# Banded attention on column halves, up-projection sums in one PSUM bank, an exchanged copy of a state-space map, reordered stick sums

## The chip, the cores and the metric

The kernel runs on one core of a Trainium2 chip. The metric is the device time of one execution in microseconds (us). The kernel before took 3503.58 us, the median of three runs (3499.01 to 3504.58).

## The reference, cut to what matters

Two transformer blocks, one after the other, on `x` of shape [1, 1024, 1024] in float32. Only the parts that the change touches are shown.

```python
# block 1: x += g_a * concat(mlstm, window_attention) @ w_out;  then a conv-GLU FFN
def window_attention(q, k, v, k_ctx, v_ctx, sink):     # 8 query heads, 2 key/value heads, 64 wide
    s_band = where(|i - j| <= 128, q . k, -inf)         # blocks of 128 queries, 3 blocks of keys
    s_ctx  = q . k_ctx                                  # 256 context keys
    p = softmax(concat([s_band, s_ctx, sink]))
    return p_band @ v + p_ctx @ v_ctx
def conv_glu(h, w_up, conv_w, conv_b, w_down):
    a, val = split(h @ w_up, 2)                         # 1024 -> 2 * 2816
    return (gelu(dwconv(a)) * val) @ w_down
# block 2: pool, dilated attention, stick-breaking attention and s5 branches, gated merge, SwiGLU FFN
def stick_breaking_attention(qkv):                      # 4 heads of 128
    log_not = where(mask, log_sigmoid(-z), 0)
    excl = reversed_cumsum(log_not) - log_not
    w = where(mask, exp(log_sigmoid(z) + excl), 0);  return w @ v
def s5_mixer(u, ...):                                   # 32 groups of 16 channels, 64 complex states
    h_t = lam_bar * h_(t-1) + b_bar @ u_t;  y = Re(c @ h) + d * u
h = silu(gu[:, :2816]) * gu[:, 2816:];  x = x + h @ w_down
```

## The kernel before

Activations lie transposed in SBUF: the 1024 features as eight tiles of 128 partitions, with the 1024 tokens along the free dimension, often cut in a left and a right half of 512. A large product is split by `split` (L378 to L388) into a rounded part `wh`/`bh` and a rest `wl`/`bl` of type fp32r, and `gemm` (L350 to L362) sums three products of these parts (L358, L360, L362). ScalarE makes the rounded part (L382) and VectorE the rest (L383). A product of plain fp32 operands is run by TensorE as two passes, and the trace lists each pass as one matmul record.

PSUM holds two tiles `mm` of two banks (`pmm`) and four tiles `ax` of one bank (`pax`). A scheduler sets the order of each engine's instructions; the code gives it generators which it runs in turns, and the pools' buffer counts decide when a tile can be written again.

**Up-projection** (`factors`, `pair`, `up`). Each 2x2 block product is done by seven half-size products instead of eight (B11, B21, T1, B22, T2, T3, T4). `factors` makes the right-hand factors from the normalised activations and `pair` the left-hand ones from the weights (`combine`, on GpSimd, L892). Every product of a pair is 4 x 3 matmuls of 128x512 and has its own PSUM bank; what is common to several results is added in SBUF: on VectorE (L900) and, for two of the seven sums, on GpSimd. A block has 22 pairs. The first two pairs run in step, since their factors are still being made; from the third on, each pair follows the one before. The norm of the right token half multiplies by the row `r` in SBUF, on VectorE for the first four tiles (L824 in block 1, L822 in block 2), on GpSimd for the last four.

**Banded attention** (`window`). There are 16 units: eight query blocks n, each for two key/value heads v. A unit makes the scores of four query heads (L1191, L1194), the softmax (L1204 to L1216), and then `values`: each block of 128 probabilities is transposed (L1229, fp32), copied to SBUF by VectorE or ScalarE (`pt`, L1232, L1234) and multiplied with 64 columns of `va` (L1236). Unit v writes to partitions 64v to 64v+63 of the bank `pv`, so it uses one half of TensorE's columns. After v = 1, L1247 spreads the reciprocal denominators with 64-column matmuls. The mLSTM runs alongside, with L1412 spreading a row of `Mn` over the partitions.

**State space** (`s5`, the loop around L2132). Per group of channels the map `RT` [128 x 128] is applied to `U` (L2132), and once more with its two column halves exchanged, as two 64-column matmuls (L2133, L2134) into the two halves of `p2`.

**Stick** (L1649 to L1673). Per key block four running sums are added in the bank `zz` before the exponential.

Of the kernel before, what the change touches and what calls it, by code (L numbers as in the profile page):

```python
# [255 lines left out]
class Kern:  # L256
# [183 lines left out]
    def rstd(self, out, acc):  # L440
        nb = out.shape[-1] // P
        y = self.rstd_tokens(acc)
        for b in range(0, nb, 4):
            n = min(4, nb - b)
            self.bcast(out[:, b * P : (b + n) * P], y[:, b : b + n])
        return self.lastr
# [365 lines left out]
    def finish(self, xs, out, gain):  # L812
# [5 lines left out]
        def norm(k, sl, eng):  # L818
            x = xs[k][:, sl]
            g, s = gain(k)  # L820
            if s is None:
                nc.vector.scalar_tensor_tensor(x, x, g, r[:, sl], ALU.mult, ALU.mult)  # L822
            else:
                eng.tensor_tensor(x, x, r[:, sl], ALU.mult)  # L824
                nc.scalar.activation(x, x, AF.Identity, scale=g, bias=s)

        B = {}
        for sl in (L, R):
# [10 lines left out]
            self.rstd(r[:, sl], acc[:, sl])  # L839
        return xd, B, self.factors(xs, B, norm)  # L840


    def factors(self, xs, B, norm):
# [13 lines left out]
        for k, (x, y) in enumerate(pairs):  # L857
            norm(k, R, nc.vector)
# [23 lines left out]
    def pair(self, fp, wa, wv, B, act):  # L882
# [3 lines left out]
        w2 = fp.tile([P, D], F32, tag="w2", name=self.nm("w2"), bufs=2)  # L886
# [3 lines left out]
        def combine(x, y, op):  # L890
            t = fp.tile([P, HT], F32, tag="ws", name=self.nm("ws"), bufs=4)
# [3 lines left out]
        def prod(ps, w, b):  # L895
            hi, lo = self.split_w(w)
            self.gemm(hi, lo, [(ps,) + B[b]])
            return ps

        add = lambda out, x, y, eng=nc.vector: eng.tensor_tensor(out, x, y, ALU.add)  # L900
        copy = lambda x, ps: nc.scalar.activation(x, ps, AF.Copy)
        ps = self.pmm()
        a = fp.tile([P, T], F32, tag="a", name=self.nm("a"), bufs=2)
        v = fp.tile([P, T], F32, tag="v", name=self.nm("v"), bufs=2)
        a0, a1, v0, v1 = a[:, 0:HT], a[:, HT:T], v[:, 0:HT], v[:, HT:T]
# [26 lines left out]
    def up(self, fp, W, B, steps, act):  # L932
        out = []
        run = lambda j: self.pair(fp, W[j], W[NF + j], B, lambda a, v: out.append(self.spill("y", act(j, a, v))))
        g = [run(0), run(1)]
# [6 lines left out]
        next(g[0])  # L942
        cur = g[1]
        for j in range(2, NF):
# [197 lines left out]
    def window(self, ep, qd, kd, kcd, va):  # L1142
# [76 lines left out]
        def values(n, v, ss, rd):  # L1219
            lo_, hi_ = span(n)  # L1220
            nk = 2 + hi_ - lo_
            hp = slice(64 * v, 64 * v + 64)
            if v == 0:
                self.pv = self.pax()
            pv = self.pv
            for k in range(nk):
                pt = self.pax()
                for j in range(4):
                    nc.tensor.transpose(pt[:, j * P : (j + 1) * P], ss[j][:, k * P : (k + 1) * P], ID)  # L1229
                t = self.wp.tile([P, 512], F32, tag="wh", name=self.nm("pt"), bufs=4)  # L1230
                if self.u % 4 == 2 or (self.u % 4 < 2 and k % 2):
                    nc.vector.tensor_copy(t, pt)  # L1232
                else:
                    nc.scalar.activation(t, pt, AF.Copy)  # L1234
                vb = va[k] if k < 2 else va[2 + lo_ + k - 2]
                self.late.append(lambda k=k, vb=vb, t=t: nc.tensor.matmul(pv[hp, :], lhsT=vb[:, hp], rhs=t, start=k == 0, stop=k == nk - 1))  # L1236
                while len(self.late) > 2:
                    self.late.pop(0)()

            while self.late:  # L1240
                self.late.pop(0)()
            if v:

                rb = self.pax()
                for g, r in enumerate((self.r0, rd)):
                    for j in range(4):
                        nc.tensor.matmul(rb[64 * g : 64 * g + 64, j * P : (j + 1) * P], lhsT=r[:, j : j + 1].to_broadcast([P, 64]), rhs=ID, start=True, stop=True)  # L1247
                rs = self.sm.tile([P, 512], F32, tag="junk", name=self.nm("rs"), bufs=1)
                nc.scalar.activation(rs, rb, AF.Copy)
                for j in range(4):  # L1250
                    t = slice(j * P, (j + 1) * P)
                    nc.vector.tensor_tensor(q[j][:, n * P : (n + 1) * P], pv[:, t], rs[:, t], ALU.mult)
            else:
                self.r0 = rd

        self.late = []
        self.qt = queries(*units[0])
        ss = scores(*units[0])
        for i, u in enumerate(units):
            self.u = i  # L1260
            nxt = scores(*units[i + 1]) if i < 15 else None
            values(*u, *ss)
# [11 lines left out]
    def mlstm(self, ep, km, kc, qm, vx, so, G):  # L1274
# [49 lines left out]
        nc.tensor.transpose(q[:, 0:128], Mn, ID)  # L1324
        nc.tensor.matmul(q[:, 128:256], lhsT=m0c.to_broadcast([P, P]), rhs=ID, start=True, stop=True)
# [20 lines left out]
        for h in range(4):  # L1346
# [56 lines left out]
            for half in range(2):  # L1403
# [4 lines left out]
                for d in range(2):  # L1408
                    pd = self.pax()
                    for j in range(4):  # L1410
                        c = col(d, blk(d, half * 4 + j + 2), h)
                        nc.tensor.matmul(  # L1412
                            pd[:, j * P : (j + 1) * P],
                            lhsT=self.c("nident")[:, c : c + 1].to_broadcast([P, P]),
                            rhs=Mn,
                            start=j == 0,
                            stop=False,
                            skip_group_check=True,
                        )
# [66 lines left out]
    def block1_ffn(self, xd, B, steps):  # L1486
        nc, tc, A = self.nc, self.tc, self.A
        with tc.tile_pool(name="f1", bufs=1) as fp:
# [3 lines left out]
            def act(j, a, v):  # L1492
# [6 lines left out]
                nc.vector.tensor_tensor(y[:, 0:HT], y[:, 0:HT], v[:, 0:HT], ALU.mult)  # L1499
                nc.gpsimd.tensor_tensor(y[:, HT:T], y[:, HT:T], v[:, HT:T], ALU.mult)  # L1500
                return y

            yd = self.up(fp, A["w_up"], B, steps, act)
# [88 lines left out]
    def stick(self):  # L1592
# [36 lines left out]
        with tc.tile_pool(name="sb", bufs=1) as fp:  # L1629
# [8 lines left out]
            def chain(h, Q, qh, ql, kh, kl, po, o):  # L1638
# [3 lines left out]
                for kb in range(kb1, -1, -1):  # L1642
# [22 lines left out]
                    if kb < kb1:  # L1665
                        pv()
                    mm(zz, ntril, Lh)
                    mm(zz, ntril, Ll, stop=kb == kb1)
                    if kb < kb1:
                        mm(zz, nones, Sh[:, c0:HT])  # L1670
                        mm(zz, nones, Sl[:, c0:HT], stop=True)
# [234 lines left out]
    def s5(self):  # L1906
# [4 lines left out]
        with tc.tile_pool(name="s5", bufs=1) as fp:  # L1911
# [143 lines left out]
            for q in range(4):  # L2055
# [32 lines left out]
                RT = v8(self.big("RT"))  # L2088
# [287 lines left out]
```

## Time and profile before

| | |
|---|---|
| median of three runs | 3503.58 us |
| the profiled execution, its span | 3506.94 us, 3505.2 us |
| mean granted TensorE clock | 0.988 |
| busy: TensorE, VectorE, ScalarE, GpSimd | 3355.7, 2239.1, 1280.0, 883.7 us |

Stages on the clock of the span, in us: projections 40 to 334, banded attention and mLSTM 334 to 600, up-projection 705 to 1138, stick 1497 to 1690, dilated attention 1763 to 2106, state space 2110 to 2460, second up-projection 2783 to 3215. A matmul record of 128x512 fp32r lasts about 0.39 us, though the next one starts earlier, because matmuls are pipelined; so a cost on TensorE is read from start to start, not from the duration of a record.

### The profile page before, as it was taken

The page shows a single profiled execution, that of the slowest core. Times are in us where ns is not written, and L with a number is a line of the kernel's source. Part 1 is how long each engine was busy: PE and PEld are TensorE (multiplying, and loading weights), DVE is VectorE, ACT ScalarE, POOL GpSimd, SP SyncE. Part 2 cuts the span into 40 slices and gives each one's busy share as a digit, 9 for nine tenths or more (in the row PEclk, how much of TensorE's full clock was granted, in tenths as well). Part 3 has the DMA queues.
Part 4 walks back from the last instruction along what each step waited for, and adds up shares of the span by engine and source line. Part 5 has one row for each costly group of instructions (what it writes and reads, how often), then busy time and mean ns, then how long its engine had stood idle before and what let it go on. Part 6 is the DMA issues. An engine that isn't in the chain of part 4 may idle for free.

```text
span 3505.2 us, 42846 instructions
## 1 busy us (share of the span) xinstructions
PE 3355.7 (96%) x15763; PEld 2644.2 (75%) x15763; DVE 2239.1 (64%) x4041; ACT 1280.0 (37%) x2410; POOL 883.7 (25%) x642
## 2 busy tenths in 40 slices
PE   6999998989999999899999999999999989999998
PEld 4797776768888777677777778777878768888767
DVE  8746776598787797667332227456265685555786
ACT  5224555443333333345232332222222333333332
POOL 3200000056555451200000002221032164544540
PEclk9999999999999999999999999999999999999999
DMA  6545111512222422200121212222464322223222
GB/s 234 193 157 174 37 52 49 174 66 79 88 75 75 165 91 85 102 25 33 54 67 46 68 57 93 70 92 75 152 228 165 126 91 84 79 84 129 94 92 78
DMA packets 139953, 348.61 MB, mean 99 GB/s; under 512 B 16712, under 2 KB 41696, under 8 KB 139744
## 3 DMA queue, kind: packets, MB, share of 16 engines
q1 hardware_dynamic: 139744, 345.88, 29.2%
q8 instruction: 124, 2.03, 0.2%
q14 instruction: 85, 0.70, 0.1%
HBM read 270.67 MB, written 75.16 MB: 99 GB/s over the span
## 4 chain that ended last, share of the span: by engine, by line
PE 80%; DVE 12%; issue 2%; DMA 2%; ACT 2%; POOL 1%; SPq 0%; DVEq 0%; ACTq 0%; POOLq 0%
PE mm L358 15%; PE mm L360 15%; PE mm L362 15%; PE ax L362 6%; PE ax L360 6%; PE ax L358 6%; DVE bl L383 2%; PE ax L1236 2%; PE ax L1649 1%; DVE wl L383 1%; PE ax L1582 1%; PE ax L1584 1%; PE ax L1583 1%; PE mm L1649 1%; PE ax L1229 1%
## 5 line engine op out<-in xcount | busy, mean ns | idle before, releaser
L382 ACT ACTIVATE wh<-w 128x512 fp32r<-128x512 f32 (+1 forms) x508 | 308.3, 610 | 1073.8 <-PE mm L360 693.0
L383 DVE TENSOR_TENSOR wl<-w,wh 128x512 fp32r<-128x512 f32 (+1 forms) x508 | 371.6, 736 | 436.3 <-ACT wh L382 393.7
L362 PE MATMUL ax<-bh,wl 128*128 128x512 f32 x928 | 369.9, 400 | 15.2 <-DVE wl L383 15.1
L360 PE MATMUL ax<-bl,wh 128*128 128x512 f32 x928 | 369.7, 398 | 5.9 <-DVE bl L383 5.7
L358 PE MATMUL ax<-bh,wh 128*128 128x512 f32 x928 | 368.4, 398 | 4.6 <-ACT bh L382 4.6
L358 PE MATMUL mm<-bh,wh 128*128 128x512 f32 x864 | 328.1, 401 | 16.7 <-DVE x L2317 6.5
L362 PE MATMUL mm<-bh,wl 128*128 128x512 f32 x864 | 321.0, 396 | 3.8 <-DVE wl L383 3.6
L360 PE MATMUL mm<-bl,wh 128*128 128x512 f32 x864 | 323.1, 395 | 0.0
L358 PE MATMUL mm<-xh,wh 128*128 128x512 f32 x944 | 311.1, 404 | 2.3 <-DVE sql L386 1.8
L362 PE MATMUL mm<-xh,wl 128*128 128x512 f32 x944 | 312.6, 403 | 0.0
L360 PE MATMUL mm<-xl,wh 128*128 128x512 f32 x944 | 305.0, 401 | 0.0
L383 DVE TENSOR_TENSOR wl<-ws,wh 128x512 fp32r<-128x512 f32 x176 | 215.5, 1234 | 32.3 <-ACT wh L382 31.9
L892 POOL TENSOR_TENSOR ws<-w 128x512 f32<-128x512 f32 x44 | 83.9, 1907 | 579.0 <-DMA w<-in_w_up_dram 508.6
L362 PEld LDWEIGHTS ax<-bh,wl 128*128 128x128 f32 x928 | 176.9, 191 | 59.7 <-DVE wl L383 19.0
L358 PEld LDWEIGHTS mm<-bh,wh 128*128 128x128 f32 x864 | 162.2, 188 | 73.4 <-DVE x L2317 12.1
L360 PEld LDWEIGHTS ax<-bl,wh 128*128 128x128 f32 x928 | 176.2, 190 | 51.8 <-DVE bl L383 11.0
L358 PEld LDWEIGHTS ax<-bh,wh 128*128 128x128 f32 x928 | 176.6, 190 | 46.2 <-ACT bh L382 6.1
L362 PEld LDWEIGHTS mm<-xh,wl 128*128 128x128 f32 x944 | 176.4, 188 | 44.5 <-issue 5.8
L358 PEld LDWEIGHTS mm<-xh,wh 128*128 128x128 f32 x944 | 174.3, 188 | 46.3 <-issue 6.3
L360 PEld LDWEIGHTS mm<-xl,wh 128*128 128x128 f32 x944 | 177.9, 189 | 40.9 <-issue 1.5
L362 PEld LDWEIGHTS mm<-bh,wl 128*128 128x128 f32 x864 | 162.6, 188 | 45.5 <-DVE wl L383 7.0
L360 PEld LDWEIGHTS mm<-bl,wh 128*128 128x128 f32 x864 | 162.9, 189 | 35.0
(636 smaller groups left out, 7101.9 us busy)
## 6 DMA issues: line engine op xcount, KB each, us to landing
w<-in_w_up_dram SPq DMA_DIRECT2D x88, 512.0 KB
wa<-in_w_ada_dram SPq DMA_DIRECT2D x64, 512.0 KB
w<-in_w_out_dram SPq DMA_DIRECT2D x32, 512.0 KB
w<-in_w_gate_dram SPq DMA_DIRECT2D x32, 512.0 KB
gd<-gf SPq DMA_DIRECT2D x32, 512.0 KB
g<-gd SPq DMA_DIRECT2D x32, 512.0 KB
y<-y SPq DMA_DIRECT2D x28, 512.0 KB
w<-in_w_down_dram SPq DMA_DIRECT2D x24, 512.0 KB
```

Source lines behind the costliest of these rows:

```text
L358: nc.tensor.matmul(ps, lhsT=wh, rhs=xh[k], start=s, stop=False, **kw)
L360: nc.tensor.matmul(ps, lhsT=wh, rhs=xl[k], start=False, stop=False, **kw)
L362: nc.tensor.matmul(ps, lhsT=wl, rhs=xh[k], start=False, stop=e, **kw)
L382: first = nc.scalar.activation(hi, src, AF.Copy)
L383: nc.vector.tensor_tensor(lo, src, hi.bitcast(F32), ALU.subtract)
L892: nc.gpsimd.tensor_tensor(t, x, y, op)
L1229: nc.tensor.transpose(pt[:, j * P : (j + 1) * P], ss[j][:, k * P : (k + 1) * P], ID)
L1236: self.late.append(lambda k=k, vb=vb, t=t: nc.tensor.matmul(pv[hp, :], lhsT=vb[:, hp], rhs=t, start=k == 0, stop=k == nk - 1))
L1582: nc.tensor.matmul(ps, lhsT=a, rhs=wh[k], start=k == 0, stop=False)
L1583: nc.tensor.matmul(ps, lhsT=a, rhs=wl[k], start=False, stop=False)
L1584: nc.tensor.matmul(ps, lhsT=b, rhs=wh[k], start=False, stop=k == KC - 1)
L1649: mm = lambda out, lhsT, rhs, **k: nc.tensor.matmul(out, lhsT=lhsT, rhs=rhs, **{"start": False, "stop": False, "skip_group_check": True, **k})
```

## The change

- `window`: the unit v = 0 is only transposed and copied (`turned`); its products wait until v = 1 is turned too, and `product` then issues for each block k the two products, one per column half. The denominators of the two heads alternate as well. The copies of v = 0 go to five buffers of their own.
- `pair`: B11, T2, T3 and T4 are summed in one bank `pa`, T1 and B22 in one bank `pb`. What stands there after B11, T1, T2 and T3 is copied out or added to SBUF before the next product is summed on top; the last sum is read from PSUM by the gate multiplication. Additions on GpSimd fall away, and `up` starts with three pairs in step.
- `factors`: the first four right-half norms read the row from the PSUM tile in which it was made (`rstd` returns it).
- `s5`: `RS`, a copy of `RT` with halves exchanged, is made by 16 more ScalarE copies, and L2133/L2134 become one 128-column matmul.
- The stick's `nones` products precede `pv()`; the mLSTM row becomes two fp32r products of a split `Mn`; a DMA scratch area gets smaller.

```diff
@@ bcast, rstd, factors
+        return ps[:, : nb * P]
-        return self.lastr
+        return row
-                nc.vector.scalar_tensor_tensor(x, x, g, r[:, sl], ALU.mult, ALU.mult)
+                nc.vector.scalar_tensor_tensor(x, x, g, row, ALU.mult, ALU.mult)
-                eng.tensor_tensor(x, x, r[:, sl], ALU.mult)
+                eng.tensor_tensor(x, x, row, ALU.mult)
-            norm(k, R, nc.vector)
+            norm(k, R, nc.vector, row)
@@ pair
+        if first is None:
+            ps = self.pmm()
+            pa, pc = ps[:, 0:HT], ps[:, HT:T]
+        else:
+            pa, pc = first
...
-        copy(a0, prod(ps[:, 0:HT], a11, "B11"))
+        prod(pa, a11, "B11", last=False)
+        copy(a0, pa)
         yield
-        p2 = prod(ps[:, HT:T], a12, "B21")
+        prod(pc, a12, "B21")
+        add(a0, pc, a0)
         yield
-        copy(v1, prod(self.pax(), s1, "T1"))
+        pb = self.pax()
+        prod(pb, s1, "T1", last=False)
+        copy(v1, pb)
+        s4 = combine(a12, s2, ALU.subtract)
         yield
-        s4 = combine(a12, s2, ALU.subtract)
-        add(a1, prod(self.pax(), s4, "B22"), v1)
-        yield
-        add(v0, prod(self.pax(), s2, "T2"), a0)
-        add(a0, p2, a0)
-        add(v1, v1, v0, nc.gpsimd)
-        add(a1, a1, v0, nc.gpsimd)
+        def p3():
+            prod(pb, s4, "B22", first=False)
+        def p6():
+            prod(pa, s2, "T2", first=False, last=False)
+            copy(a1, pa)
...
+        add(a1, pb, a1)
+        y = hidden(a) if first is None else None
         yield
-        s3 = combine(a11, a21, ALU.subtract)
-        p7 = prod(self.pax(), s3, "T3")
-        add(v1, p7, v1)
-        add(v0, p7, v0)
+        prod(pa, s3, "T3", first=False, last=False)
+        add(v1, pa, v1)
         yield
-        add(v0, prod(self.pax(), a22, "T4"), v0)
-        act(a, v)
+        prod(pa, a22, "T4", first=False)
+        out(y or hidden(a), pa, v1)
@@ up
+        def gated(y, v0, v1):
+            nc.vector.tensor_tensor(y[:, 0:HT], y[:, 0:HT], v0, ALU.mult)
+            nc.vector.tensor_tensor(y[:, HT:T], y[:, HT:T], v1, ALU.mult)
+        p, q = self.pmm(), self.pmm()
+        g = [run(0, (p[:, 0:HT], q[:, HT:T])), run(1, (p[:, HT:T], None)), run(2, (q[:, 0:HT], None))]
-        g = [run(0), run(1)]
@@ window
+            def product(k, t1):
+                vb = va[k] if k < 2 else va[2 + lo_ + k - 2]
+                for v, t in enumerate((t0[k], t1)):
+                    hp = slice(64 * v, 64 * v + 64)
+                    nc.tensor.matmul(pv[hp, :], lhsT=vb[:, hp], rhs=t, start=k == 0, stop=k == nk - 1)
...
+            if v == 0:
+                t0, r0 = [turned(n, 0, ss[0], k) for k in range(blocks(n))], ss[1]
+            else:
+                values(n, t0, ss[0], (r0, ss[1]))
@@ s5
-                        R = RT[:, 4 * j + g, :]
-                        nc.tensor.matmul(p1[:, o], lhsT=R, rhs=U[:, 4 * j + g, :], start=True, stop=True)
-                        nc.tensor.matmul(p2[0:64, o], lhsT=R[:, 64:128], rhs=U[:, 4 * j + g, :], start=True, stop=True)
-                        nc.tensor.matmul(p2[64:128, o], lhsT=R[:, 0:64], rhs=U[:, 4 * j + g, :], start=True, stop=True)
+                        for p, R in ((p1, RT), (p2, RS)):
+                            nc.tensor.matmul(p[:, o], lhsT=R[:, 4 * j + g, :], rhs=U[:, 4 * j + g, :], start=True, stop=True)
```

The first place is TensorE's order in the banded attention, at the end of unit n = 2. In the kernel before, `pt` are the turned probabilities of head v = 1, L1229 the transposes, L1247 the denominators:

```order
L1236 MATMUL ax_3505<-pt_3661,va_1271 64x512
L1229 MATMUL ax_3679<-const,ws_3463 128x128
L1229 MATMUL ax_3679<-const,ws_3472 128x128
L1229 MATMUL ax_3679<-const,ws_3481 128x128
L1229 MATMUL ax_3679<-const,ws_3490 128x128
L1236 MATMUL ax_3505<-pt_3668,va_1331 64x512
L1247 MATMUL ax_3689<-const,rden_3316 64x128 x4
L1236 MATMUL ax_3505<-pt_3676,va_1361 64x512
L1236 MATMUL ax_3505<-pt_3684,va_1391 64x512
L1247 MATMUL ax_3689<-const,rden_3503 64x128 x4
```

In the changed kernel L1259 are the transposes and L1282 the products; of the `pt` of one `va` the lower number belongs to v = 0, the higher to v = 1:

```order
L1282 MATMUL ax_3665<-pt_3539,va_1271 64x512
L1282 MATMUL ax_3665<-pt_3678,va_1271 64x512
L1259 MATMUL ax_3698<-const,ws_3485 128x128
L1259 MATMUL ax_3698<-const,ws_3494 128x128
L1259 MATMUL ax_3698<-const,ws_3503 128x128
L1259 MATMUL ax_3698<-const,ws_3512 128x128
L1282 MATMUL ax_3665<-pt_3546,va_1331 64x512
L1282 MATMUL ax_3665<-pt_3685,va_1331 64x512
L1282 MATMUL ax_3665<-pt_3553,va_1361 64x512
L1282 MATMUL ax_3665<-pt_3694,va_1361 64x512
L1282 MATMUL ax_3665<-pt_3560,va_1391 64x512
L1282 MATMUL ax_3665<-pt_3703,va_1391 64x512
```

Products of the head v = 0 no longer stand among the transposes of their own unit but directly ahead of the product of v = 1 with the same `va`, in the other column half.

The second place is VectorE's order at the start of the first up-projection, from the norm of the right token half on. In the kernel before, L824 is the norm, L846 makes T1, `bl` is the rest of a factor, `wl` that of a weight:

```order
L824 TENSOR_TENSOR x_5477<-x_5477,r_5486 128x512
L824 TENSOR_TENSOR x_5478<-x_5478,r_5486 128x512
L824 TENSOR_TENSOR x_5479<-x_5479,r_5486 128x512
L824 TENSOR_TENSOR x_5480<-x_5480,r_5486 128x512
L846 TENSOR_TENSOR t_1327_6330<-x_5477 128x512
L869 TENSOR_TENSOR x_5477<-x_5477 128x512
L383 TENSOR_TENSOR bl_6333<-t_1327_6330,bh_6332 128x512
L846 TENSOR_TENSOR t_1330_6338<-x_5478 128x512
L846 TENSOR_TENSOR t_1331_6344<-x_5479 128x512
L869 TENSOR_TENSOR x_5478<-x_5478 128x512
L383 TENSOR_TENSOR bl_6333<-t_1330_6338,bh_6332 128x512
```

In the changed kernel L826 is the norm, L848 makes T1 and L903 adds a product of the pairs 1 to 3 (`a`) from PSUM:

```order
L826 TENSOR_TENSOR x_5547<-x_5547,ax_6299 128x512
L826 TENSOR_TENSOR x_5548<-x_5548,ax_6299 128x512
L383 TENSOR_TENSOR wl_6430<-w_6366,wh_6429 128x512
L826 TENSOR_TENSOR x_5549<-x_5549,ax_6299 128x512
L848 TENSOR_TENSOR t_1339_6448<-x_5547 128x512
L826 TENSOR_TENSOR x_5550<-x_5550,ax_6299 128x512
L383 TENSOR_TENSOR bl_6451<-t_1339_6448,bh_6450 128x512
L848 TENSOR_TENSOR t_1342_6456<-x_5548 128x512
L848 TENSOR_TENSOR t_1343_6462<-x_5549 128x512
L903 TENSOR_TENSOR a_6316<-mm_6311,a_6316 128x512
L383 TENSOR_TENSOR wl_6476<-ws_6318,wh_6475 128x512
L903 TENSOR_TENSOR a_6343<-ax_6410,a_6343 128x512
```

The norm's second operand moved from `r` to a PSUM tile, and the parts for three pairs' weights and the additions of their B21 now stand between the steps that make T1.

## Rows read from the trace of the kernel before

**Rows 1.** Page, busy time of each engine, with its share and instructions.

```profile
PE 3355.7 (96%) x15763; PEld 2644.2 (75%) x15763; DVE 2239.1 (64%) x4041; ACT 1280.0 (37%) x2410; POOL 883.7 (25%) x642
```

**Rows 2.** Windows of two stages: length, busy us (instructions) of PE, PEld, DVE, ACT, POOL; clock; DMA.

```profile
334.00:600.00 266.00, 248.07 (x1607) 181.26 (x1605) 186.50 (x572) 143.55 (x404) 0.00 (x0) 0.99 0.13 43
2110.00:2450.00 340.00, 337.76 (x1600) 270.87 (x1599) 216.01 (x643) 80.78 (x140) 73.76 (x84) 0.98 0.26 84
```

**Rows 3.** Groups by line, 334 to 600: busy us, mean ns, idle before.

```profile
L1236 PE MATMUL ax<-pt,va 128*64 128x512 f32 x152 | 74.8, 606 | 3.4 <-ACT pt L1234 2.1 <-ACT kw L1374 1.2
...
L1412 PE MATMUL ax<-Mn,const 128*128 128x128 f32 x128 | 17.8, 282 | 2.8 <-ACT dt L1428 2.7
```

**Rows 4.** Timeline of TensorE at 348: start, duration, line, tiles, count.

```profile
348.83 1.07 PE L1236 MATMUL ax<-pt,va 128*64 128x512 f32 x2 [0.22 <-ACT pt L1234]
349.83 0.66 PE L1229 MATMUL ax<-const,ws 128*128 128x128 f32 x4
```

**Rows 5.** Timeline of TensorE at 364, with both column halves at work.

```profile
364.10 0.62 PE L1229 MATMUL ax<-const,ws 128*128 128x128 f32 x4
364.65 0.64 PE L1236 MATMUL ax<-pt,va 128*64 128x512 f32 x1
364.66 0.65 PE L1247 MATMUL ax<-const,rden 128*64 128x128 f32 x4
...
365.56 1.02 PE L1236 MATMUL ax<-pt,va 128*64 128x512 f32 x2
366.42 0.27 PE L1247 MATMUL ax<-const,rden 128*64 128x128 f32 x1
```

**Rows 6.** Waits of TensorE, 334 to 600: sum, times, longest.

```profile
PE mm L1191 <- DVE mx L1204: 3.9, 7, 2.0
```

**Rows 7.** Timeline of TensorE at 2230, one group of the state-space map.

```profile
2230.01 0.49 PE L2132 MATMUL ax<-U,RT 128*128 128x128 f32 x2
2230.43 0.32 PE L2133 MATMUL ax<-U,RT 128*64 128x128 f32 x1
...
2230.59 0.27 PE L2133 MATMUL ax<-U,RT 128*64 128x128 f32 x1
...
2230.80 0.49 PE L2132 MATMUL ax<-U,RT 128*128 128x128 f32 x2
```

**Rows 8.** Groups by line on ScalarE, 2110 to 2450.

```profile
L2095 ACT ACTIVATE RT<-ax 128x512 f32<-128x512 f32 x8 | 4.8, 598 | 18.2 <-PE ax L2093 18.2
```

**Rows 9.** Windows of the two up-projections: start, and then full rate, in equal lengths.

```profile
705.00:795.00 90.00, 73.60 (x293) 55.32 (x292) 81.43 (x97) 43.09 (x67) 53.21 (x33) 0.92 0.20 68
795.00:885.00 90.00, 90.00 (x390) 72.92 (x389) 71.60 (x75) 33.32 (x51) 54.22 (x34) 1.00 0.23 83
2780.00:2860.00 80.00, 66.37 (x259) 49.46 (x258) 69.58 (x90) 31.95 (x55) 42.33 (x26) 0.91 0.18 63
2860.00:2940.00 80.00, 80.00 (x347) 64.83 (x346) 47.29 (x61) 26.96 (x43) 41.22 (x29) 1.00 0.26 93
```

**Rows 10.** Waits of TensorE at the first start, 700 to 770.

```profile
PE ax L362 <- DVE wl L383: 5.2, 3, 2.6
PE ax L360 <- DVE bl L383: 4.7, 3, 2.2
```

**Rows 11.** Groups by line on VectorE at the first start, 700 to 770.

```profile
L824 DVE TENSOR_TENSOR x<-x,r 128x512 f32<-128x512 f32 x4 | 5.8, 1506 | 1.3 <-ACT r L431 1.3
...
L900 DVE TENSOR_TENSOR a<-ax,v 128x512 f32<-128x512 f32 x2 | 1.4, 676 | 0.0
```

**Rows 12.** Groups by line on VectorE at the second start, 2780 to 2860.

```profile
L822 DVE SCALAR_TENSOR_TENSOR x<-x,smalls,r 128x512 f32<-128x512 f32 x8 | 6.7, 873 | 1.9 <-ACT r L431 1.9
```

**Rows 13.** Waits of VectorE in the steady part of the first up-projection, 800 to 1100.

```profile
DVE v L900 <- PE ax L362: 37.7, 32, 1.4
```

**Rows 14.** Groups by line on VectorE in the same stretch.

```profile
L1496 DVE SCALAR_TENSOR_TENSOR y<-a,fcw,y 128x1023 f32<-128x1023 f32 x15 | 19.3, 1284 | 8.8 <-ACT y L1495 8.8
```

**Rows 15.** Waits of TensorE in the stick, 1495 to 1690.

```profile
PE mm L1649 <- ACT w L1673: 0.8, 3, 0.3
```

More of the change, by code (lines that the diff above doesn't have):

```diff
@@ L878, in factors, with pair @@
         yield
-    def pair(self, fp, wa, wv, B, act):
+    def pair(self, fp, wa, wv, B, hidden, out, first=None):
         nc = self.nc
@@ L885, in pair @@
         nc.sync.dma_start(w, wa)
[L886 removed]
+        w2 = fp.tile([P, D], F32, tag="w2", name=self.nm("w2"), bufs=3)
         nc.sync.dma_start(w2, wv)
@@ L941, in up @@
         next(steps)
-        next(g[0])
-        cur = g[1]
-        for j in range(2, NF):
+        for i in g:
+            next(i)
+        cur = run(3)
+        for _ in range(6):
+            next(cur)
+        for j in range(4, NF):
             new = run(j)
@@ L1217, in scores @@
             return ss, r
[L1219 to L1225, printed above, removed]
-            for k in range(nk):
[L1227 to L1254, printed above, removed]
@@ L1256, in window, with turned @@
-        self.late = []
+        def turned(n, v, ss, k):
+            pt = self.pax()
+            for j in range(4):
+                nc.tensor.transpose(pt[:, j * P : (j + 1) * P], ss[j][:, k * P : (k + 1) * P], ID)
+            if v:
+                t = self.wp.tile([P, 512], F32, tag="wh", name=self.nm("pt"), bufs=4)
+            else:
+                t = self.mp.tile([P, 512], F32, tag="pt", name=self.nm("pt"), bufs=5)
+            if (n % 2 and not v) or (not n % 2 and k % 2):
+                nc.vector.tensor_copy(t, pt)
+            else:
+                nc.scalar.activation(t, pt, AF.Copy)
+            return t
@@ new lines, in window, with values @@
+        blocks = lambda n: 2 + span(n)[1] - span(n)[0]
+        def values(n, t0, ss, rds):
+            lo_, nk = span(n)[0], blocks(n)
+            pv = self.pax()
+            late = []
+            def product(k, t1):
[3 more added lines that the diff above has]
+                    nc.tensor.matmul(pv[hp, :], lhsT=vb[:, hp], rhs=t, start=k == 0, stop=k == nk - 1)
+            for k in range(nk):
+                late.append((k, turned(n, 1, ss, k)))
+                if len(late) > 2:
+                    product(*late.pop(0))
+            for a in late:
+                product(*a)
+            rb = self.pax()
+            for j in range(4):
+                for g, r in enumerate(rds):
+                    nc.tensor.matmul(rb[64 * g : 64 * g + 64, j * P : (j + 1) * P], lhsT=r[:, j : j + 1].to_broadcast([P, 64]), rhs=ID, start=True, stop=True)
+            rs = self.sm.tile([P, 512], F32, tag="junk", name=self.nm("rs"), bufs=1)
+            nc.scalar.activation(rs, rb, AF.Copy)
+            for j in range(4):
+                t = slice(j * P, (j + 1) * P)
+                nc.vector.tensor_tensor(q[j][:, n * P : (n + 1) * P], pv[:, t], rs[:, t], ALU.mult)
@@ L1324, in mlstm @@
         nc.tensor.transpose(q[:, 0:128], Mn, ID)
+        nid, Mh, Ml = (ep.tile([P, P], F32R, name=n) for n in ("nid", "Mh", "Ml"))
+        nc.vector.tensor_copy(nid, self.c("nident"))
+        self.split(Mn, Mh, Ml)
         nc.tensor.matmul(q[:, 128:256], lhsT=m0c.to_broadcast([P, P]), rhs=ID, start=True, stop=True)
@@ L1411, in mlstm @@
                         c = col(d, blk(d, half * 4 + j + 2), h)
[L1412 to L1419, printed above, removed]
+                        for i, part in enumerate((Mh, Ml)):
+                            nc.tensor.matmul(
+                                pd[:, j * P : (j + 1) * P],
+                                lhsT=nid[:, c : c + 1].to_broadcast([P, P]),
+                                rhs=part,
+                                start=j == 0 and i == 0,
+                                stop=False,
+                                skip_group_check=True,
+                            )
                     it = self.sm.tile([P, 512], F32, tag="it", name=self.nm("it"), bufs=2)
```

75 lines of the change are left out of this document (42 added, 33 removed).

## The prediction

> **What bounds the kernel now.** I read the busy line of the page first: TensorE is busy 3355.7 of 3505.2 us, every other engine at most 64% [rows 1]. So an edit pays where it takes passes from TensorE or ends a stop of TensorE, and the next question is which stages stop. Equal windows answer it. At full rate an up-projection runs 390 matmuls in 90 us, 0.231 us each, with TensorE busy throughout; its starts run 293 in 90 us and 259 in 80 us where full rate is 347 [rows 9]. That is (390 - 293) x 0.231 = 22.4 us lost at the first start and 88 x 0.231 = 20.3 us at the second. The state-space stage is busy 337.76 of 340 us, so there only passes count. Banded attention with the mLSTM is busy 248.07 of 266 us, VectorE 186.50 and ScalarE 143.55 [rows 2]: passes count, and the other engines have some room. For the price of a pass I then read timelines, start to start; for the stops, the waits by line.
>
> **Banded attention.** The products L1236 are 152 records, 76 matmuls of two passes [rows 3]. Two passes in a row take 366.42 - 365.56 = 0.86 us, 0.43 each [rows 5]. One alone among transposes takes 1.00 us to the next instruction [rows 4], so 0.14 us more for changing between 64 and 128 columns. That two column halves work at once this trace shows: a pass of L1236 starts at 364.65 and four denominators of the other half at 364.66 [rows 5].
>
> In the order after, two products with the same weights stand side by side, one per half. TensorE takes instructions in order and each product needs its two passes one after the other in its own half. So in a stretch of m alternating products the second pass of one runs beside the first of the next: m + 1 slots of 0.43 us and not 2m. I counted the stretches of 64-column work in the order of the change: 27, holding all 76 products, from one to six each; before there are 43. Slots: 76 + 27 = 103 and not 152, 49 x 0.43 = 21 us. From that I take what before already has side by side, the denominators under a product at the end of the eight query blocks, 0.5 to 0.7 us each as in [rows 5]: -5. The 16 stretches that go away save at least one change each, 16 x 0.14 = 2.2, twice that if the change into a stretch costs the same: +3. That is 19 us. What is late next: all products now come after the second head's copies, five at a time, and behind a product that waits stand the scores of the next unit, for which VectorE (70% busy) waits. TensorE's longest sum of waits there is 3.9 us now [rows 6]; I give 2 of the 19 back. **-17**. Bounds: changes alone and nothing side by side, -2; 21 + 4.5 = -25 with all of it.
>
> The Trainium skill, TensorEngine Tiling (Array Packing), Key Properties, says that different tiles can load weights and multiply in parallel, and that changing the mode drains the engine. The starts 0.01 us apart and the 0.14 us agree with it. By independence alone, with both halves filled all the time, the products would need 76 slots and the saving would be 76 x 0.43 = 33 us; here the order of a single queue keeps it to the 103 slots above.
>
> **mLSTM row.** One fp32 matmul of two passes becomes two fp32r matmuls: 128 records before [rows 3], 128 after. **0**, between -7 (half of 128 passes of 0.11 us, were the weights not loaded again) and +2 for the split at its head.
>
> **State space.** A group before: two passes of L2132 start at 2230.01, the halves at 2230.43 and 2230.59, the next group at 2230.80 [rows 7]: 0.79 us, of which a good part is changing width twice. After, four 128-column passes and no change of width. Four such passes take 364.65 - 364.10 = 0.55 us with a change behind them [rows 5]; less 0.10 for that change 0.45. 32 groups x (0.79 - 0.45) = **-11**; with 0.55, 32 x 0.24 = -8. The 16 added copies are at most 16 x 0.598 = 9.6 us of ScalarE [rows 8], which is busy 80.78 of 340 us [rows 2]; they stand ahead of the group's products, so if that cover were gone, up to 9.6 of the gain would go.
>
> **Starts of the up-projections.** Three pairs start in step and not two. While the norm and T1 are made, TensorE has the products B11 and B21 of three pairs, six of 12 x 0.231 = 2.8 us each, and not four: 5.6 us more cover at either start. VectorE holds what comes next; the two waits on its `wl` and `bl` are 9.9 us of the first start [rows 10]. The four norms of the right half take 1506 ns each from SBUF, while an operation with a PSUM operand takes 676 ns in the same stretch [rows 11]. So 4 x 0.83 = 3.3 us come off the first start, and 8 x (0.873 - 0.676) = 1.6 off the second [rows 12]. The additions that leave GpSimd and VectorE I put at 1 us a start, since VectorE makes the same number of parts between norm and last T4 factor, now for three pairs. First start 5.6 + 3.3 + 1 = **-10**, second 5.6 + 1.6 + 1 = **-8**. Bounds: -3 each (norms, or a little of the cover, alone) and -17 (three quarters of the loss). New: pair 4 needs the banks of pairs 1 and 2, so its B11 waits until their gate multiplications are through; behind it stands nothing else on TensorE. I count that inside the -10.
>
> **Steady pairs.** 84 matmuls a pair before and after, at full rate with no stop [rows 9]: no gain possible. New waits: T2, T3 and T4 may start only when the sum before them has been read out of the same bank. The order puts B22 between T2 and T3 and the next pair's B11 between T3 and T4, 2.8 us each, and the read is one ScalarE copy or VectorE addition of about 0.7. VectorE now arrives early at such sums: it waits 37.7 us for TensorE there, 32 times [rows 13]. **0**. Only the last pair has no next pair: 1 us in each block, **+2**.
>
> **Stick and the rest.** The same matmuls in another order; the waits there are 0.8 us and less [rows 15]. **-1** (0 to -4). The smaller scratch moves no instruction: 0.
>
> **Sum.** -17 + 0 - 11 - 10 - 8 + 0 + 2 - 1 = -45 us against the profiled 3506.94: 3462. That execution stands 3.4 us above the median of the runs shown, so I forecast **3459 us**.
>
> **Rivals.**
> 1. The halves don't run side by side when both stream 512 columns: then the banded attention gives only the changes of width, -3, and the sum is -31: 3473. For it: no row shows two 512-column products at once. Against: one of 512 runs beside four of 128 [rows 5].
> 2. The starts gain nothing: VectorE is busy 81.43 of 90 us there [rows 9] and has the same number of operations, and TensorE, with more products in step, waits later for T3 and T4. Then -17 - 11 - 1 + 2 = -27: 3477. Against: the same VectorE time now feeds 252 matmuls and not 168.
> 3. The starts recover nearly all that TensorE can use, -17 and -15: sum -59, 3445. For it: 42.7 us are lost there, and the clock is granted at 0.92 and 0.91 on average [rows 9], which more work in a row may bring back to 1. Against: VectorE has hardly any room there.
> 4. Slower: the shared bank stops TensorE in every pair. In 36 steady pairs T3 waits for a copy and T4 for an addition. If VectorE stands in one 1.28 us convolution step and a `wl` when T3 ends [rows 14], and the addition behind them comes 2 us after the cover of 2.8 is used up, each pair loses 2 us, and with 0.6 at T3 2.6: 36 x 2.6 = 94 us, less 45: 3553. It decides from 45 / 36 = 1.25 us a pair. Against: the waits of VectorE for TensorE in [rows 13]. The Trainium skill, PSUM — Partial Sum Buffer, on bank collisions, says that two engines may not be at one bank at a time and that reads should target another bank than the running matmul; it speaks for this rival, since the change gives up one bank per product, and the trace of before, where each product has its own, cannot show the price.
>
> **How the numbers follow.** Forecast 0.5, rival 1 0.12, rival 2 0.17, rival 3 0.14, rival 4 0.04, the rest (mishaps that leave it within a few us of before) 0.03. The range from 3425 to 3488 takes in rivals 1 to 3 and the bounds: all terms at their better end (-25 - 11 - 17 - 17 - 7 - 4 and nothing lost, -81) give 3423, and -8 for the state space, -6 for both starts, and -5 for banded attention give -17, 3487. About 7 us (0.2%) is what a measurement can tell from no change. Faster by more: 0.92. Within: 0.03. Slower by more: 0.05.
>
> **What would show it.** In the profile after: L1282 in pairs starting about 0.01 us apart or with the second pass beside the next product's first, and the stretch from the first scores to the last product some 17 us shorter; groups of the state-space map 0.45 us apart; at the two starts, more than 293 matmuls in the first 90 us and norms of about 0.7 us; between pairs no wait of T3 or T4. The forecast is wrong if TensorE waits for L903 or for copies of `pa` in every pair, or if the products of the banded attention start 0.43 us apart without overlap.

## The result, and the profile after

The changed kernel takes 3455.03 us (median of four runs, 3452.84 to 3456.07), the kernel before 3502.97 (3499.01 to 3504.58): a ratio of 0.9864, 95% interval 0.9847 to 0.9881, so 48 us less. The forecast was 3459 us. The total came out, but two of its terms did not, and that they made up for each other was luck.

The two profiled executions stand 54 us apart (3506.94 and 3452.84), since the first lies 4 us above its median and the second 2 below. The table gives, for some matmuls that both programs issue, how much earlier they start after; the second column is the same program profiled once more (e11).

| start of | before, us | change | again (e11) |
|---|---|---|---|
| norm row, left half, before up-projection 1 | 666.5 | -30.4 | -28.8 |
| norm row, right half | 713.8 | -26.3 | -27.5 |
| norm row behind down-projection 1 | 1396.8 | -29.5 | -32.6 |
| first stick matmul | 1497.7 | -30.4 | |
| last dilated product | 2105.7 | -34.3 | |
| last state-space map | 2424.4 | -43.7 | |
| norm row, right half, up-projection 2 | 2790.9 | -44.8 | -47.5 |
| norm row behind down-projection 2 | 3470.2 | -53.9 | -56.5 |

So up to the first up-projection 30 us came, 27 of them in the stage of the banded attention, where 17 were forecast; the first up-projection gave between +0.9 and -3.8, forecast -9 with its tail; the state space about -9, forecast -11; the second up-projection -9, forecast -7 with its tail. The rest is 6 us of small differences, 4 of them between the first stick matmul and the last dilated product.

One trace of either kernel measures an up-projection badly, since its clock differs from run to run. Four kernels have the up-projection of before (before, e1, e3, e4) and five that of the change (the change, e2, e5, e6, e11). The table has their means and, in brackets, the lowest and the highest, in us, from the norm row of the left half (first) or of the right half (second) to the norm row behind the down-projection. Idle is the length less TensorE's busy time; half clock is the time at the lower level of the granted clock, 1.2 and not 2.4 GHz.

| | length | idle | half clock |
|---|---|---|---|
| first, as before | 732.6 (730.3 to 734.6) | 28.6 (27.5 to 30.1) | 19.6 (17.1 to 23.9) |
| first, changed | 729.4 (726.6 to 731.3) | 25.0 (24.2 to 26.6) | 20.5 (13.7 to 27.3) |
| second, as before | 678.9 (678.7 to 679.3) | 25.4 (24.4 to 26.3) | 18.8 (17.1 to 20.5) |
| second, changed | 670.6 (670.1 to 671.7) | 21.7 (21.0 to 22.3) | 8.9 (6.8 to 10.2) |

The length less the idle time and less half of the time at half clock is the same with and without the change: 693.3 to 695.4 us in the nine traces of the first, 643.9 to 645.2 in those of the second. So the first gained 3 us, all of it idle time. The second gained 8: 4 are idle time and 5 are clock. Why the clock stays up at the second and not at the first, no run shows.

**Page and windows after**, in the columns of [rows 1], [rows 2] and [rows 9]. The stretch 334 to 574 answers to 334 to 600 before. The windows of the two starts lie as far from the norm row of the left half (first) and of the right half (second) as those of before.

```profile
PE 3312.0 (96%) x15699; PEld 2635.8 (76%) x15699; DVE 2092.2 (61%) x3955; ACT 1311.0 (38%) x2471; POOL 654.7 (19%) x510
```

```profile
334.00:574.00 240.00, 220.01 (x1607) 173.07 (x1605) 184.97 (x580) 146.82 (x409) 0.00 (x0) 0.98 0.15 49
674.60:764.60 90.00, 77.22 (x299) 58.90 (x298) 78.75 (x97) 44.91 (x71) 44.55 (x28) 0.91 0.19 67
775.00:865.00 90.00, 90.00 (x390) 72.90 (x389) 54.77 (x67) 37.12 (x56) 25.83 (x20) 1.00 0.23 82
2735.20:2815.20 80.00, 69.76 (x287) 53.74 (x286) 67.09 (x91) 35.28 (x60) 34.61 (x23) 0.96 0.19 61
```

The banded attention issues the same 1607 matmuls in 26 us less, with 28 us less of TensorE's busy time: passes lie side by side. The first start runs 299 matmuls in 90 us and not 293 (308 in e11), at a clock of 0.91 and not 0.92; the second 287 in 80 us and not 259, at 0.96 and not 0.91. Full rate is the same 390 as before.

**Timeline of TensorE in the banded attention after**: start, duration, line, tiles, count of records, to be read beside [rows 4].

```profile
390.85 1.08 PE L1282 MATMUL ax<-pt,va 128*64 128x512 f32 x4
391.86 0.66 PE L1259 MATMUL ax<-const,ws 128*128 128x128 f32 x4
```

Four records, which is two products of two passes, take 391.86 - 390.85 = 1.01 us to the next instruction. In [rows 4] one product took 1.00. The single records start at 390.853 and 390.860, then at 391.333 and 391.340: the first passes of both heads run together, then the second passes. Over the stage 62 passes start within 0.01 us of one of the other head; before, none does. So 152 passes fill 90 slots, 62 with two passes and 28 with one.

**Timeline of TensorE in the state space after**, to be read beside [rows 7].

```profile
2193.55 0.38 PE L2183 MATMUL ax<-U,RT 128*128 128x128 f32 x2
2193.77 0.39 PE L2183 MATMUL ax<-U,RS 128*128 128x128 f32 x2
2194.00 0.39 PE L2183 MATMUL ax<-U,RT 128*128 128x128 f32 x2
```

A group takes 2194.00 - 2193.55 = 0.45 us, as worked out.

**Waits of TensorE at the first start after**, 670 to 762, to be read beside [rows 10].

```profile
PE ax L421 <- DVE acc L413: 2.4, 1, 2.4
PE mm L358 <- ACT a L904: 2.4, 1, 2.4
PE ax L360 <- DVE bl L383: 2.1, 3, 1.0
...
PE mm L358 <- DVE y L962: 1.5, 1, 1.5
PE mm L358 <- DVE v L903: 1.3, 1, 1.3
PE mm L362 <- DVE wl L383: 0.9, 2, 0.6
```

The 9.9 us of waits for `wl` and `bl` shrank to 3.0. In their place stand four that before did not have at this size: the sum of squares (L421), the copy out of the shared bank ahead of the next product (L904), and the banks of pairs 1 to 3, which pair 4 and the T4 products need (L962, L903): 7.6 us.

In the steady parts, 760 to 1110 and 2826 to 3172, TensorE waits for nothing. From 770 to 1080 VectorE still waits for the shared bank's sums and not the other way round:

```profile
DVE a L903 <- PE ax L362: 27.2, 16, 1.7
```

### The profile page after: what moved, and what is told of

Same layout as the page of the kernel before. It is cut to its first block, busy times and chain, and to the rows that moved or that the text cites. A ratio compares the mean times of both kernels' runs of the same rounds, so it can differ in the third digit from the quotient of the medians.

```text
span 3451.0 us, 42496 instructions
## 1 busy us (share of the span) xinstructions
PE 3312.0 (96%) x15699; PEld 2635.8 (76%) x15699; DVE 2092.2 (61%) x3955; ACT 1311.0 (38%) x2471; POOL 654.7 (19%) x510
## 5 line engine op out<-in xcount | busy, mean ns | idle before, releaser
L358 PE MATMUL mm<-bh,wh 128*128 128x512 f32 x1376 | 532.9, 401 | 26.7 <-ACT a L904 6.2
L362 PE MATMUL mm<-bh,wl 128*128 128x512 f32 x1376 | 523.6, 396 | 4.0 <-DVE wl L383 3.8
L360 PE MATMUL mm<-bl,wh 128*128 128x512 f32 x1376 | 526.3, 396 | 0.2 <-DVE bl L383 0.2
L358 PEld LDWEIGHTS mm<-bh,wh 128*128 128x128 f32 x1376 | 259.8, 189 | 110.2 <-DVE x L2364 11.7
L362 PEld LDWEIGHTS mm<-bh,wl 128*128 128x128 f32 x1376 | 259.7, 189 | 68.7 <-DVE wl L383 7.6
L360 PEld LDWEIGHTS mm<-bl,wh 128*128 128x128 f32 x1376 | 260.0, 189 | 57.8 <-DVE bl L383 0.6
L358 PEld LDWEIGHTS mm<-xh,wh 128*128 128x128 f32 x944 | 174.3, 188 | 44.8 <-issue 5.1
L382 ACT ACTIVATE wh<-ws 128x512 fp32r<-128x512 f32 x176 | 110.7, 630 | 202.0 <-PE mm L360 171.9
L362 PE MATMUL ax<-bh,wl 128*128 128x512 f32 x416 | 165.3, 397 | 4.2 <-DVE wl L383 4.2
L360 PE MATMUL ax<-bl,wh 128*128 128x512 f32 x416 | 165.9, 399 | 2.2 <-DVE bl L383 2.1
L358 PE MATMUL ax<-bh,wh 128*128 128x512 f32 x416 | 165.8, 398 | 1.6 <-ACT bh L382 1.6
```

The costliest lines, as they stand in the source:

```text
L358: nc.tensor.matmul(ps, lhsT=wh, rhs=xh[k], start=s, stop=False, **kw)
L360: nc.tensor.matmul(ps, lhsT=wh, rhs=xl[k], start=False, stop=False, **kw)
L362: nc.tensor.matmul(ps, lhsT=wl, rhs=xh[k], start=False, stop=e, **kw)
L382: first = nc.scalar.activation(hi, src, AF.Copy)
```

## The experiments

Each was timed beside the kernel before. The first four are the kernel before with one part of the change, and with its smaller DMA scratch area.

**e1, the banded attention alone** (`turned`, `values` and the loop over the units as in the change).

> The kernel before with the banded attention of the change alone. Theory: the two column halves work side by side, and the stage from 334 us to the last product shrinks by about 30 us (25 us of products, 5 us of denominators, both read start to start in the trace after, and more than the 27 us of the whole change, because the mLSTM row cost something there): 3503 - 30 = 3473 us. Rival: the halves bring what was forecast, 17 us (3486), and the remaining 10 us of that stage come from the mLSTM row.

3471.11 us, ratio 0.9903 (0.9889 to 0.9916): 33 us less. From the first scores to the last product it takes 233.6 us and not 266.4. Start to start the products go from 65.2 us to 43.4, the denominators from 14.7 to 9.7, the transposes from 47.5 to 44.7. The theory holds. The rival wanted 10 us of the stage from the mLSTM row; this kernel has not got the row, and its stage is 6 us shorter than that of the change (239.8 us).

**e2, the up-projection alone** (`pair`, `up`, `factors`, the norm row).

> The kernel before with the up-projection of the change alone (one bank, three pairs in step, norm row from PSUM). Theory from the two traces: the first start gains nothing (0 to -3 us), the second 9 us: 3503 - 10 = 3493 us. Rival, the forecast: 10 and 8 us less 2 at the tails: 3503 - 16 = 3487 us, and the first start in the trace after was lost to something else that this kernel does not have.

3498.99 us, ratio 0.9986 (0.9978 to 0.9995): 5.5 us less. From the left norm row on, the first up-projection is 1.0 us longer than in the trace of before and 1.3 shorter than the mean of the four kernels that have it as before; the second, from its right norm row on, is 9.3 and 8.8 shorter. The interval of the ratio, 2 to 8 us, leaves out the rival (16 us) and the theory (10) as well: less came than either says. In its trace the program ahead of the left norm row, which is that of before, took 4.2 us longer, and that hides part of the 10; whether it did so in the other runs, nothing shows. So the rival is out, and the size of the theory is shown by the trace alone.

**e3, the state space alone** (`RS` and its products).

> The kernel before with the state-space edit alone. Theory: 32 groups at 0.45 us and not 0.79: -11 us at most, 3492 us; the landmarks of the trace after give -8 to -9. Rival: the 16 copies on ScalarE are not hidden and take up to 9.6 us back: 3501 us.

3498.79 us, ratio 0.9984 (0.9975 to 0.9992): 5.7 us less. In its trace 8.5 us come between the dilated attention and the gated merge, and 6 were lost before the stage, where the program is the same. The interval, 3 to 9 us, leaves out the 11 of the theory, and the median lies nearer to the rival. What speaks against the rival is the trace: 8.5 us came in the stage, and TensorE doesn't wait for a copy there.

**e4, the mLSTM row alone.**

```diff
-   nc.tensor.matmul(pd[...], lhsT=self.c("nident")[:, c : c + 1].to_broadcast([P, P]), rhs=Mn, ...)
+   for i, part in enumerate((Mh, Ml)):
+       nc.tensor.matmul(pd[...], lhsT=nid[:, c : c + 1].to_broadcast([P, P]), rhs=part, ...)
```

> The kernel before with the mLSTM row alone (two fp32r products of a split row and not one fp32 product). Theory: it costs about 5 us, because the row takes 23.6 us of TensorE, start to start, in the trace after and 16.2 before, and the mask matmul behind it 1.3 and not 3.6: 3508 us. Rival, the forecast: 0, 3503 us.

3538.59 us, ratio 1.0097 (1.0081 to 1.0112): 34 us more, seven times what the theory said. Its stage, waits and then window (columns as above):

```profile
PE mm L1191 <- DVE mx L1204: 11.1, 14, 2.1
PE ax L1483 <- DVE hid L1476: 8.3, 3, 2.8
```

```profile
334.00:637.00 303.00, 268.80 (x1619) 197.59 (x1617) 189.26 (x574) 145.02 (x405) 0.00 (x0) 0.92 0.13 41
```

A pass costs 0.11 us in either form. The order is another: TensorE has three rows of 32 to 36 score matmuls, where the longest before is 20, and they stand where VectorE has not yet made room for them ([rows 6]: 3.9 us before, 11.1 here). The clock, granted at 0.99 before [rows 2], is 0.92, with seven stretches at half clock that last 48 us where before has one of 6.8. In the window TensorE is idle 34 us and not 18, which is 16 of the 34 us; 41 us more at half clock are, by the account above, 20. That the order is the cause is argued from this, since no run changes the order alone; the scratch area is not it, since e1 to e3 have it too.

**e5, the whole change without the row.**

> The whole change without the mLSTM row (one fp32 product as before). Alone the row cost 34 us, with the same price of 0.11 us a pass in both traces, so its cost lies in waits that the newly made order brings. Theory: in the change it costs the 6 us that TensorE waits there for the exponentials before the mask matmul, and this kernel takes 3450 us. Rival: in the order of the change the row is free or a help, 3455 us or more.

3451.94 us, ratio 0.9849 (0.9836 to 0.9863), 3 us below the change. The intervals overlap, so the medians don't tell this kernel from the change. The stage takes 235.5 us and not 239.8: the row, with the mask matmul behind it, goes from 24.9 us to 17.1, the products take 44.7 and not 39.8. In this order the row costs 4 us of the stage: 8 at the row itself, less 5 at the products, of which 62 passes run beside another with the row and 56 without it. The sign fits the theory; in the medians it is not shown.

**e6, products by head.**

```diff
+   for k in range(nk):
+       vb = va[k] if k < 2 else va[2 + lo_ + k - 2]
+       nc.tensor.matmul(pv[0:64, :], lhsT=vb[:, 0:64], rhs=t0[k], start=k == 0, stop=k == nk - 1)
    for k in range(nk):
        late.append((k, turned(n, 1, ss, k)))
...
-       for v, t in enumerate((t0[k], t1)):
-           hp = slice(64 * v, 64 * v + 64)
-           nc.tensor.matmul(pv[hp, :], lhsT=vb[:, hp], rhs=t, ...)
+       nc.tensor.matmul(pv[64:128, :], lhsT=vb[:, 64:128], rhs=t1, ...)
```

> The whole change, but in the banded attention the products of head v = 0 all stand ahead of those of v = 1: the same instructions, half by half and not alternating. Theory (passes of two halves run side by side): the 49 slots of 0.43 us come back, about 20 us, 3475 us. Rival (the gain comes from fewer changes of width and from products that no longer wait for their copies): at most 4 us more, 3459 us.

3489.59 us, ratio 0.996 (0.9946 to 0.9973), 34.6 us above the change. No two products run together any more, and they take 62.2 us start to start and not 39.8: the 22 us of the theory. The rival is out. The stage is 276.7 us long and not 239.8. Of these 37 us, 5 are idle time and 5 are clock (20.5 us at half clock and not 10.2); what is left, 27, is 62 passes of 0.43 us. New is a wait of 7.1 us for `pt` behind v = 0, here by line (busy us, mean ns, idle before):

```profile
L1280 PE MATMUL ax<-pt,va 128*64 128x512 f32 x76 | 40.0, 608 | 7.1 <-ACT pt L1267 7.1
L1284 PE MATMUL ax<-pt,va 128*64 128x512 f32 x76 | 35.6, 601 | 0.0
```

The 0.6 us a record is the same when two run at once; only the starts tell.

**e7, two pairs in step and not three.**

```diff
-   g = [run(0, (p[:, 0:HT], q[:, HT:T])), run(1, (p[:, HT:T], None)), run(2, (q[:, 0:HT], None))]
+   g = [run(0, (p[:, 0:HT], p[:, HT:T])), run(1, (q[:, 0:HT], q[:, HT:T]))]
```

> The whole change with two pairs in step at the starts of the up-projections and not three. Theory (two more products as cover while T1 is made): the second start is 5 to 6 us longer; the first start is unchanged within 2 us, because what the third pair gives there is taken back by its additions on GpSimd, which slow the sum of squares: 3461 us. Rival: the norm row and the additions that fall away make the gain, and nothing changes: 3455 us.

3461.22 us, ratio 0.9874 (0.9861 to 0.9888), 6 us above the change, with intervals that overlap. In the traces the second up-projection gains 4.2 us over before and not 9.1, the first 0.0. In the second TensorE is idle 24.5 us, little less than without the change, and 13.7 us are at half clock (in the change 21.7 and 8.9 on average). In the first it is idle 23.7 us, no more than with the third pair. So the third pair is worth 5 us at the second start, half of it idle time and half clock, beside the 5.6 of the forecast, and no idle time at the first.

**e8, the third pair's additions held back** until the norm row is there (`gate` is set for that pair).

```diff
+            if gate and x is a21:
+                nc.gpsimd.tensor_copy(t[:, 0:1], self.rrow[:, HT : HT + 1])
             nc.gpsimd.tensor_tensor(t, x, y, op)
```

> The whole change, with the third pair's first two additions on GpSimd held back by a copy of one column until the norm row of the right half is there. Theory (these additions slowed VectorE's last sum of squares by 2.6 us, TensorE then waited 2.8 us and its clock fell to half for 6.8 us): the first start gains 3 to 6 us, 3450 us. Rival: GpSimd then does its norms later and the parts for B22 are late, nothing gained or up to 4 us lost.

3454.01 us, ratio 0.9858 (0.9845 to 0.9871): not to be told from the change. In the trace the wait for the sum of squares is gone, and the first up-projection gains 2.9 us over before; the second gains 7.3 and not 9.1. What held up the sum of squares shows in the change, VectorE first, then GpSimd:

```profile
670.95 2.83 DVE L383 TENSOR_TENSOR bl<-x,bh 128x512 fp32r<-128x512 f32 x2
673.71 1.78 DVE L413 TENSOR_TENSOR acc<-acc,sq 128x512 f32<-128x512 f32 x1
...
670.14 1.39 POOL L896 TENSOR_TENSOR ws<-ws,w 128x512 f32<-128x512 f32 x1 [2.20 <-DMA w<-in_w_up_dram]
671.49 3.44 POOL L896 TENSOR_TENSOR ws<-w,ws 128x512 f32<-128x512 f32 x2
```

Before, the same two VectorE steps took 1.28 and 0.69 us, with GpSimd idle. The 2.6 us reach TensorE: its sum of squares starts at 680.69, 2.83 us behind the matmul before it, and a stretch of 6.8 us at half clock begins right there. In e11, the same program, the wait is there too (2.5 us), and the next stretch at half clock begins 23 us later; so that the wait brings the clock down is not shown. Nor is a cost: with the third pair held back the waits for `bl` and `wl` grow to 3.6 and 2.5 us (2.1 and 0.9 in the change), and TensorE is idle 26.1 us in the first up-projection, 24.6 in e9, where the five traces of the change have 24.2 to 26.6.

**e9, e5 and e8 together, held back in block 1 alone.**

> The whole change without the mLSTM row, and with the third pair's additions on GpSimd held back in the first block alone. Theory: the two gains add, 3 us from the row (4 us in its stage) and 3 to 4 us at the first start, where holding back gave 3.8 us, while it took 1.8 us at the second start: 3448 us. Rival: the gain at the first start was a matter of where the half-clock stretches fell and does not come again: 3452 us.

3451.17 us, ratio 0.985 (0.9837 to 0.9864): ahead of the kernel before by 53 us, and not to be told from e5 or from the change. The median lies by the rival (3452), and whether the two gains add stays open; its profiled execution (3446.09 us) was the shortest of a wide spread, up to 3457.48.

**e10, the norm from SBUF.**

```diff
-            norm(k, R, nc.vector, row)
+            norm(k, R, nc.vector)
```

> The whole change, but the first four norms of the right half read the row from SBUF again. Theory (an operation with two SBUF operands takes up to 1.77 us beside GpSimd, one with a PSUM operand 0.68): the norms take about 1.5 and 0.9 us each again and both starts are 2 to 4 us and 1 to 2 us longer: 3459 us. Rival: the wait for other parts sets the pace and nothing changes: 3455 us.

3461.76 us, ratio 0.9874 (0.9858 to 0.989), 6.8 us above the change beside it (e11), with intervals that overlap a little. The first up-projection is 3.8 us longer than in the trace of before, the second 4.9 shorter: 3 to 8 and 4 us worse than the change. The norms of the first start by line, here and in e11:

```profile
L826 DVE TENSOR_TENSOR x<-x,r 128x512 f32<-128x512 f32 x4 | 4.9, 1235 | 4.4 <-ACT r L431 4.4
```

```profile
L826 DVE TENSOR_TENSOR x<-x,ax 128x512 f32<-128x512 f32 x4 | 2.6, 681 | 1.9 <-ACT r L431 1.9
```

Saved on VectorE itself: 4 x (1235 - 681) ns = 2.2 us. TensorE is idle 27.4 us in this up-projection and 25.0 in the traces of the change, so these 2 us reach it. At the second start it is otherwise. In block 2 VectorE makes all eight norms of the right half, not only the first four. Only those four read PSUM in the change, and VectorE takes as long for two of them from SBUF, in e10, as from PSUM, in the change:

```profile
2755.99 1.41 DVE L824 SCALAR_TENSOR_TENSOR x<-x,smalls,r 128x512 f32<-128x512 f32 x2 [1.88 <-ACT r L431]
```

```profile
2747.89 1.41 DVE L824 SCALAR_TENSOR_TENSOR x<-x,smalls,ax 128x512 f32<-128x512 f32 x2 [1.88 <-ACT r L431]
```

So the 4 us at the second start are not the price of the norms. They are 1 us more of idle time and 13.7 us at half clock and not 8.9; what brings them stays open.

**e11, the change again.**

> The change itself once more, as the measure for the two others on the same chip: 3455 us. Its first up-projection start should again show no gain over the kernel before (0 to 1 us), and its second 9 us.

3454.99 us, ratio 0.9856 (0.9842 to 0.9869). The second up-projection gains 9.0 us once more. The first gains 3.8 where the first profile lost 0.9: the same program, idle 25.2 us here and 24.2 there, but with 13.7 us at half clock here and 27.3 there. So one profile tells the first start only to some 5 us, and "no gain" was too firm; the means above give 3 us.

## Why the prediction was right, point by point

- **What bounds**: right. TensorE stays at 96%, and the gain came from passes, from stops of TensorE and, at the second up-projection, from its clock.
- **Banded attention, -17**: the mechanism was right, its size was not. The step that failed is "the second pass of one runs beside the first of the next: m + 1 slots". The trace after shows first beside first and second beside second: a pair takes two slots, not three. 62 passes fell away, 62 x 0.43 = 26.7 us, and the 103 slots of the forecast were 90. Counted two by two, the 27 stretches give 88, since 12 of them hold an odd number of products. The other 28 passes ran alone. The Trainium skill, TensorEngine Tiling (Array Packing), Key Properties, says that tiles work in parallel, and the starts agree. By it alone there would have been 76 slots and 33 us; the 90 lie midway between that and the single queue that I set against it. The -5 for what the kernel before "already has side by side" was wrong as well: the products cost 0.43 us a pass before too (65.2 us for 152), and the denominators, which I left out, gave 5 us of their own. The stage gave 33 us alone and 27 with the row. Rival 1 is out by e6.
- **mLSTM row, 0**: wrong in kind. The passes cost what I said, but the edit has the scheduler make a new order, and I priced only the passes. 34 us alone (e4); in the change 4 us of the stage, which the medians don't show (e5).
- **State space, -11**: 0.45 us a group as worked out, with 0.10 taken off for the change of width that stood in no row; 9 us came. In the change TensorE waits 3.4 us there for the products that follow (L2195), 0.9 before.
- **First start, -10**: mis-sized; about 3 us came. The term that failed is the 5.6 us of cover: without the third pair TensorE is idle for no longer there (e7, 23.7 us). The waits that I named shrank by 7 us, but four others took their place: "pair 4 needs the banks ... I count that inside" had a size, 1.5 and 1.3 us, and the copy out of the shared bank and the sum of squares had 2.4 each. The norm row was worth 2 us (e10), where I had 3.3. The third pair's additions on GpSimd stretch VectorE's sum of squares from 0.69 to 1.78 us, but holding them back gains nothing that the runs tell (e8).
- **Second start, -8**: -8 to -9, but in good part by luck. The third pair brought 5 (e7), where I had 5.6 of cover, and half of that is clock; of the whole gain 5 us are clock, which I priced nowhere but in rival 3. The 1.6 for the norms was a misreading: of the eight norms of [rows 12] only the first four read PSUM after, and they take 0.7 us each from either place (e10).
- **Steady pairs, 0**: right. Rival 4 is out: no wait in 36 pairs. The tail, +2, was at most 0.4 us: the last pair of the first block waits that long for a read of the shared bank, that of the second doesn't. So one bank costs nothing where a product of 2.8 us stands between the sum and the next product on top of it.
- **Stick, -1**: first to last matmul 190.0 us and not 191.1.

Too little in one term (10 us) and too much in another (7) gave the right total, and that is luck. Rival 2 is out, since the idle time fell at both starts by more than its spread. The bounds do not quite fit the range: their better end, 3423, lies 2 us outside it.

## What to carry to other kernels

Look at how matmuls on two column halves of the array start, not how long their records last: issued next to each other they ran pass by pass together, and a pair cost what one did. A shared accumulation bank costs nothing in a steady loop whose next product covers the read, and shows up where the loop starts. Read TensorE's idle time and its time at half clock apart, and over several traces: the idle time showed a gain of 3 us that the length of one trace could not. And an edit that leaves every price alone can still cost one per cent if a scheduler makes a new order from it: look at the order and at the waits of the stage, not only at the instruction.

## What the runs showed that I had not expected

- Two fp32 products of two passes each, on different column halves, run in lockstep: starts 7 ns apart, 1.01 us for two and 1.00 for one.
- One edit without a price (e4) moved the kernel by 34 us, with 48 us at half clock in its stage and not 6.8.
- The same program's first up-projection differed by 5 us between two profiled executions, with 27.3 and 13.7 us at half clock.
- Of the 8 us that the second up-projection gained, 5 are clock.
